# A planner's lag between dependent instructions of one engine, in a one-core hybrid decoder step

## The chip, the cores and the metric

The kernel runs on one core of one Trainium2 chip, as one launch. The metric is device time in microseconds (us), and the median of a few runs counts. Engine names are those of the profile: PE is TensorE's matmul side and PEld its weight loads, DVE is VectorE, ACT ScalarE, POOL GpSimd, SP SyncE; SPq is the queue on which SP issues its DMAs.

## The reference: what is computed

One layer of a decoder step for a prompt of 1024 tokens and 8 single-token samples, width 1024. The stream is normalised and modulated (adaLN), projected by `w_in` into parts, and sent to two groups of heads:

- an mLSTM with 4 heads of 128: a matrix memory carried over chunks of 128 tokens, each head's output normalised per token;
- sparse attention with 8 query heads of 64 and 2 key-value heads, in three branches (compressed blocks, the top 16 selected blocks, a window of 512), each a masked softmax with a relative-position bias, merged by sigmoid gates.

```python
parts, gate = adaln_project(x_p, c_prompt, w_ada, b_ada, w_in, b_in)
hm, (C_p, n_p, m_p) = mlstm_mixer(qm, km, vm, om, im, fm, m_norm_g, carry0, M_CHUNK)
ha = nsa_prompt(qa, cmp_p, slc_p, win_p, ga, cmp_params, rel_bias)
mix = concatenate([hm * silu(zm), ha * silu(za)], axis=-1)
x_p = layer_norm(DEEPNORM_ALPHA * x_p + gate * (mix @ w_out + b_out), ln_g, ln_b)
```

The samples go the same way against paged caches of 2048 rows each. Besides both streams the kernel returns the new key-value rows and the mLSTM's states.

## The kernel before

All of it is one program. Its stages overlap: the compression of the samples' cache, adaLN and normalisation (0 to 155 us of the span); the input projection, 35 blocks of up to 128 columns, each a matmul in three parts of split float32 (tile `mm`, from 110 to 914 us), which also serves as filler between other work; the samples' attention (232 to 363 us); the prompt's attention in 32 units (352 to 790 us); the four mLSTM heads (504 to 913 us); the output projection in 8 tiles of 128 tokens (from 914 us).

**The order is written by a planner, in Python, while the program is built.** Every piece of work is a generator, a *lane*, with a rank. `Lanes.run` (L326) takes, at each turn, the first lane in rank whose next step is ready by the planner's PE clock plus `SLACK` (0.2 us, L138), or else the one ready soonest, and lets it emit one step. The instructions then stand in that order in each engine's queue; an engine does not overtake, and waits by semaphore where a result isn't there yet. The planner's clocks never reach the chip; only the order does, and a few choices of engine: `sooner` (L506) gives an operation to the engine whose clock (plus a stated cost) is lowest, as in `sooner((V, 0.6), (G, 1.2))` for the products and the low halves of the output tiles (`mix_load`, L2355, and `split`, L518).

`Plan.note` (L247) keeps those clocks, one for each of PE, DVE, ACT, POOL and DMA (SP's queue). An instruction starts at the latest of its engine's clock and its waits. One kind of wait is read after write: for each part of a tile that it reads, the end of whatever wrote it, plus a lag given by `after` (L218): `LAG` of the writer's engine plus `TO` of the reader's. A step's readiness for PE is the latest `after(e, "PE")` of what it emitted (`step_end`), or the end of named tiles. A DRAM tile counts as one part, and a DMA that reads it waits for the DMAs that wrote it. The costs of an instruction are formulas: 0.069 us + n/960 for most DVE operations of n elements, 0.15 us + (n-1)/475 or /195 on POOL.

Steps that are named below:

- `mlstm_norm` (L1568), run 8 times (`mn00` to `mn31`): on DVE a chain of 13 instructions on `den`, `mst`, `mmv` and `mva` after the head's `nd`; then a reciprocal square root (`rsqrt_steps`, L475), 15 instructions on POOL for seven of the runs and 12 on DVE for the last; then `mva` and `nd` on DVE, PE transposes of `nd`, and `qm`.
- `finish` (L2233), run 9 times: the last layer norm, with a reciprocal square root of 9 instructions on DVE (`rs_v`, `rs_y`, `rs_t`, `frs`).
- DRAM tiles as ways between steps: `ud` to `ur` (`bias_tables`, L1790), `gpd` to `gate` (`out_gate`, L2267), and `mxd` and `gtd` to `mix` (`mix_load`).

Of the kernel before, what the change touches and what calls it, by code (L numbers as in the profile page):

```python
# [143 lines left out]
class Plan:  # L144
# [2 lines left out]

    LAG = {"PE": 0.2, "ACT": 0.15, "DVE": 0.13, "POOL": 0.08, "DMA": 0.0}
    TO = {"PE": 0.07, "POOL": 0.03}
    TICK = 10.24 / 3  # L150

    def __init__(self):
# [12 lines left out]
    def pe_cost(self, t, op, out, ins):  # L165
# [6 lines left out]
        else:  # L172
            cyc, passes = max(2 * n, 2 * m), 2
        tick = int(t / self.TICK)
        full = self.columns.get(tick - 1, 0) >= 3060
# [42 lines left out]
    def after(self, e, kind):  # L218
        return e[0] + self.LAG[e[1]] + self.TO.get(kind, 0.0)

# [26 lines left out]
    def note(self, kind, op, a, kw):  # L247
        aps = [x for x in a if isinstance(x, bass.AP)] + [x for k, x in kw.items() if isinstance(x, bass.AP)]
        out = kw.get("out", a[0] if a else None)
        outs = [out] + ([kw["accum_out"]] if "accum_out" in kw else [])  # L250
        if "in_offset" in kw and kw["in_offset"] is not None:
            aps.append(kw["in_offset"].ap)
        ins = list(aps)
        for o in outs:
            ins.pop(next(i for i, x in enumerate(ins) if x is o))
        eng = kind
        waits = [(self.clock[kind], kind, "")]
        for x in ins:
            for c in self.cells(x):
                for e in self.wrote.get(c, ()):  # L260
                    if not (kind == "PE" and e[1] == "PE"):
                        waits.append((self.after(e, kind), e[1], c))
        for x in aps:
            if x.space == PSUM or any(x is o for o in outs):
                for c in self.cells(x):
                    waits += [(self.after(e, kind), k, c) for k, es in self.used.get(c, {}).items() if k != kind
                              for e in es]
        load = kind == "DMA" or op == "indirect_dma_start"
        if load and len(self.begun[kind]) >= 8:
            waits.append((self.begun[kind][-8][0], "RING", ""))  # L270
        t = max(w[0] for w in waits)
        if load:
            size = out.free_size() * 4 * out.partition_size() / 360.0e3
            run = min(x.ap[-1][1] if x.ap[-1][0] == 1 else 1 for x in [out] + ins)
            if run < 128 and kind == "DMA":
                size *= 2
            self.clock[kind] = t + (1.04 if kind == "POOL" else 0.475)
            eng = "DMA"
            e = [0.0, eng]
            self.transfer(self.clock[kind] + 0.65, size, e)  # L280
            self.begun[kind].append(e)
        else:
            c = self.cost(kind, op, t, out, ins, len(outs) > 1)
            e = [t + c, kind]
            eng = kind
            self.clock[kind] = t + c
            self.step_end = max(self.step_end, self.after(e, "PE"))
        for x in outs:
            for c in self.cells(x):
                self.wrote[c] = (self.wrote.get(c, []) if eng == "DMA" else [])[-7:] + [e]  # L290
        for x in aps:
            for c in self.cells(x):
                u = self.used.setdefault(c, {})
                u[eng] = (u.get(eng, []) if eng == "DMA" else [])[-7:] + [e]
# [2176 lines left out]
```

## Time and profile before

| | |
|---|---|
| median of 3 runs | 1039.39 us (1038.61 to 1039.49) |
| the profiled execution | 1039.46 us, span 1037.6 us, mean granted TensorE clock 0.967 |
| PE busy | 959.7 us, 92% of the span |
| DVE, ACT, POOL busy | 717.2, 530.2, 286.5 us |
| chain that ended last | PE 57%, DVE 11%, DMA 4% of the span |

Span and busy times come from one profiled execution; 1.9 us lie around its span. The granted clock is 1.00 where TensorE ran at 2.4 GHz all the time and 0.50 where it ran at 1.2 GHz. A row of the view by stages gives each engine's busy time in that stretch, with the number of instructions in brackets; a row of the timeline gives start, length, engine, operation and tiles (out<-in), and in square brackets how long the engine had been idle and what released it.

### The profile page before, as it was taken

What the parts mean: (1) busy time and instruction counts of PE and PEld (TensorE: products, weight loads), DVE (VectorE), ACT (ScalarE), POOL (GpSimd) and SP (SyncE); (2) the same over time, 40 slices, a digit from 0 to 9 for tenths busy, and PEclk for the clock granted to TensorE, in tenths of its full rate; (3) what the DMA queues carried; (4) which work ended last, traced back from release to release, by engine and by line L of the source; (5) the groups of instructions that cost most, each with busy time, mean ns of one, the idle gap of its engine ahead of it and who ended that gap; (6) DMA issues with size and microseconds to landing.
All of it is one profiled execution on the core that took longest, in us unless ns stands there. A gap on an engine that the chain in (4) does not pass through costs nothing.

```text
span 1037.6 us, 20058 instructions
## 1 busy us (share of the span) xinstructions
PE 959.7 (92%) x7338; PEld 864.9 (83%) x7338; DVE 717.2 (69%) x2266; ACT 530.2 (51%) x1329; POOL 286.5 (28%) x362
## 2 busy tenths in 40 slices
PE   4997899999999989999999999999999899989990
PEld 3786897989888889899999998899998889967780
DVE  4859864072323477789777788878784738999996
ACT  3557752143344656676667786666773321231111
POOL 6216423111453000110131001131012524253563
PEclk9988899999999989999999999999999989989996
DMA  8943419413698715311105111012102326479502
GB/s 329 408 189 117 148 70 361 151 50 118 221 326 286 216 55 165 111 57 37 47 11 157 29 47 38 25 36 74 47 33 85 113 65 191 142 264 362 168 22 81
DMA packets 85334, 141.42 MB, mean 136 GB/s; under 512 B 11657, under 2 KB 58286, under 8 KB 85108
## 3 DMA queue, kind: packets, MB, share of 16 engines
q1 hardware_dynamic: 76020, 106.59, 31.2%
q0 software_dynamic: 9216, 33.56, 9.0%
q8 instruction: 58, 0.95, 0.4%
q14 instruction: 40, 0.33, 0.1%
HBM read 117.73 MB, written 28.15 MB: 141 GB/s over the span
## 4 chain that ended last, share of the span: by engine, by line
PE 57%; DVE 11%; DMA 4%; issue 2%; POOL 2%; ACT 1%; POOLq 0%; SPq 0%; DVEq 0%; ACTq 0%
PE mm L308 27%; PE sc L308 13%; PE tp L308 9%; PE oo L308 7%; DVE xr L308 2%; DMA wof<-in_w_out 1%; DMA pgs<-in_cache_slc_kv,idx 1%; DVE smp L308 1%; DVE lnst L308 1%; DVE rs_t L308 1%; POOL wol L308 1%; DMA mg<-mgd 1%; DVE mixl L308 1%; DMA pgs<-in_cache_win_kv 1%; DVE rs_y L308 0%
## 5 line engine op out<-in xcount | busy, mean ns | idle before, releaser
L308 PE MATMUL mm<-hh,wh 128*128 128x344 f32 (+1 forms) x840 | 286.3, 341 | 0.0
L308 PE MATMUL mm<-hl,wh 128*128 128x344 f32 (+1 forms) x840 | 270.4, 322 | 0.0
L308 PE MATMUL mm<-hh,wl 128*128 128x344 f32 x816 | 262.6, 322 | 0.0
L308 POOL TENSOR_TENSOR wl<-wf,wh 128x1024 fp32r<-128x1024 f32 (+1 forms) x35 | 82.5, 2356 | 505.0 <-ACT wh L308 389.6
L308 PEld LDWEIGHTS mm<-hh,wh 128*128 128x128 f32 (+1 forms) x840 | 158.8, 189 | 12.1 <-issue 10.5
L308 PEld LDWEIGHTS mm<-hl,wh 128*128 128x128 f32 (+1 forms) x840 | 158.9, 189 | 0.7
L308 PEld LDWEIGHTS mm<-hh,wl 128*128 128x128 f32 x816 | 155.1, 190 | 0.0
L308 PE MATMUL oo<-pt,VT 128*64 128x128 f32 x1056 | 70.1, 276 | 0.0
L308 PE MATMUL sc<-kst,qs 128*128 128x448 f32 (+6 forms) x208 | 69.5, 343 | 0.3 <-DVE pt L308 0.3
L308 PE MATMUL sc<-kst,ql 128*128 128x448 f32 (+6 forms) x208 | 65.5, 325 | 0.0
L308 PEld LDWEIGHTS oo<-pt,VT 128*64 128x64 f32 x1056 | 58.1, 137 | 6.4 <-issue 5.2
L308 DVE COPY pt<-tp 128x512 f32<-128x512 f32 (+1 forms) x87 | 54.8, 645 | 9.9 <-PE tp L308 9.7
L308 ACT ACTIVATE pw<-pw,nbs 128x64 f32<-128x64 f32 (+2 forms) x112 | 54.6, 489 | 12.6 <-DVE tot L308 6.4
L308 ACT ACTIVATE pt<-tp 128x512 f32<-128x512 f32 (+1 forms) x73 | 39.8, 558 | 40.6 <-PE tp L308 40.4
L308 ACT ACTIVATE pa<-pa,nbs 128x384 f32<-128x384 f32 (+1 forms) x88 | 50.9, 580 | 14.6 <-DVE pa L308 12.4
L308 ACT ACTIVATE xh<-tp 128x512 fp32r<-128x512 f32 x64 | 38.0, 595 | 35.2 <-PE tp L308 34.9
L308 DVE TENSOR_TENSOR xl<-tp,xh 128x512 fp32r<-128x512 f32 x64 | 42.8, 679 | 14.3 <-ACT xh L308 14.0
L308 PE MATMUL tp<-KA,pgx 128*128 128x128 f32 x256 | 43.3, 293 | 2.8 <-ACT pgx L308 1.9
L308 ACT ACTIVATE ti<-sc,PKT 128x129 f32<-128x129 f32 x28 | 10.3, 369 | 67.3 <-DVE cx L308 67.3
L308 ACT ACTIVATE pp<-pp,nbs 128x64 f32<-128x64 f32 (+3 forms) x72 | 32.2, 449 | 22.7 <-DVE nbs L308 21.3
L308 PE MATMUL sc<-xl,w1h 128*128 128x256 f32 x128 | 38.3, 299 | 5.0 <-DVE xl L308 5.0
L308 PEld LDWEIGHTS sc<-kst,qs 128*128 128x128 f32 x208 | 39.8, 191 | 3.3 <-DVE pt L308 1.0
(506 smaller groups left out, 2285.0 us busy)
## 6 DMA issues: line engine op xcount, KB each, us to landing
wf<-in_w_blk SPq DMA_DIRECT2D x34, 512.0 KB
wada<-in_w_ada SPq DMA_DIRECT2D x24, 512.0 KB
wof<-in_w_out SPq DMA_DIRECT2D x16, 512.0 KB
xt<-in_x_prompt SPq DMA_DIRECT2D x8, 512.0 KB
pgs<-in_cache_win_kv SPq DMA_DIRECT2D x8, 512.0 KB
qf<-qtd SPq DMA_DIRECT2D x32, 128.0 KB
mix<-mxd SPq DMA_DIRECT2D x16, 256.0 KB
mix<-gtd SPq DMA_DIRECT2D x16, 256.0 KB
```

The source lines that it names most:

```text
L308: return f(*a, **kw)
```

## The change

The planner gets a table `OWN`, and the read-after-write wait of an instruction on its own engine's result is counted with it in place of `LAG` and `TO`:

```diff
     LAG = {"PE": 0.2, "ACT": 0.15, "DVE": 0.13, "POOL": 0.08, "DMA": 0.0}
     TO = {"PE": 0.07, "POOL": 0.03}
+
+    OWN = {"ACT": 0.1, "DVE": 0.09, "POOL": 0.08}
...
         for x in ins:
             for c in self.cells(x):
                 for e in self.wrote.get(c, ()):
-                    if not (kind == "PE" and e[1] == "PE"):
+                    if e[1] != kind:
                         waits.append((self.after(e, kind), e[1], c))
+                    elif kind in self.OWN:
+                        waits.append((e[0] + self.OWN[kind], kind, c))
```

In the code before, the wait on the engine's own result is counted too, by `after`: 0.15 us for ACT, 0.13 us for DVE, 0.08 + 0.03 = 0.11 us for POOL. It becomes 0.10, 0.09 and 0.08 us. For PE none is counted, before or after. A DMA that reads what a DMA wrote had its wait counted with a lag of 0; DMA is not in `OWN`, so the planner now counts no wait there. No instruction is added or removed, and the semaphores on the chip follow the data as before.

## Rows read from the trace of the kernel before

**Rows 1.** Busy time by stage: stretch, its length, engines, PE's granted clock, DMA.
```profile
815.00:830.00 15.00, 10.82 (x64) 10.32 (x63) 11.17 (x22) 5.07 (x9) 9.30 (x18) 0.88 0.03 10
830.00:845.00 15.00, 15.00 (x93) 14.98 (x92) 4.33 (x11) 0.00 (x0) 2.21 (x1) 0.90 0.23 75
845.00:860.00 15.00, 12.46 (x97) 11.64 (x96) 8.59 (x35) 7.16 (x15) 4.16 (x5) 0.79 0.42 121
915.00:925.00 10.00, 6.69 (x19) 4.79 (x18) 9.80 (x18) 3.25 (x4) 6.97 (x3) 0.67 0.80 254
940.00:1012.00 72.00, 72.00 (x344) 56.33 (x343) 67.95 (x129) 12.91 (x16) 36.92 (x17) 1.00 0.51 169
```

**Rows 2.** Waits of PE: engine, tile <- releaser: us in total, times, longest.
```profile
PE tp L308 <- DVE nd L308: 5.9, 2, 4.2
PE oo L308 <- DVE gx L308: 3.1, 3, 1.5
PE sc L308 <- DVE vs L308: 3.0, 1, 3.0
PE tp L308 <- DVE d L308: 2.5, 1, 2.5
```

**Rows 3.** Timeline of DVE: four that don't depend on each other, then a chain.
```profile
1.20 0.34 DVE L308 TENSOR_SCALAR m<-io 128x1 f32<-128x1 int32 x4
...
1003.06 0.14 DVE L308 TENSOR_SCALAR rs_v<-fmv 128x1 f32<-128x1 f32 x1
1003.24 0.15 DVE L308 TENSOR_SCALAR rs_y<-rs_v 128x1 int32<-128x1 int32 x1
...
1004.96 0.16 DVE L308 SCALAR_TENSOR_TENSOR fnm<-fmv,frs 128x1 f32<-128x1 f32 x1
```

**Rows 4.** Timeline of POOL in the reciprocal square root of one `mlstm_norm`.
```profile
822.27 1.14 POOL L308 TENSOR_TENSOR rs_t<-rs_t,rs_v 128x4 f32<-128x4 f32 x1
823.50 0.23 POOL L308 TENSOR_SCALAR rs_t<-rs_t 128x4 f32<-128x4 f32 x1
823.81 0.20 POOL L308 TENSOR_TENSOR rs_y<-rs_t,rs_y 128x4 f32<-128x4 f32 x1
...
826.10 0.20 POOL L308 TENSOR_TENSOR mva<-rs_t,rs_y 128x4 f32<-128x4 f32 x1
```

**Rows 5.** Timeline of DVE around the same `mlstm_norm`.
```profile
812.90 1.83 DVE L308 SCALAR_TENSOR_TENSOR den<-nd 128x4 f32<-128x4 f32 x1
814.76 2.32 DVE L308 TENSOR_TENSOR den<-den,PKT 128x4 f32<-128x4 f32 x1
...
826.33 1.20 DVE L308 TENSOR_TENSOR mva<-mva,den 128x4 f32<-128x4 f32 x1 [2.98 <-POOL mva L308]
```

**Rows 6.** Timeline of PE, its transposes of `nd` in two runs of `mlstm_norm`.
```profile
827.97 1.25 PE L308 MATMUL tp<-KA,nd 128*128 128x128 f32 x4 [4.18 <-DVE nd L308]
...
912.27 0.84 PE L308 MATMUL tp<-KA,nd 128*128 128x128 f32 x3 [1.72 <-DVE nd L308]
```

**Rows 7.** Waits of SP's queue on a DMA's landing, where that DMA wrote DRAM.
```profile
SPq L308 <- DMA ud<-ut: 2.7, 1, 2.7
SPq L308 <- DMA gtd<-to: 2.0, 1, 2.0
SPq L308 <- DMA gpd<-smp: 0.9, 1, 0.9
SPq L308 <- DMA qtd<-qt: 0.8, 1, 0.8
```

**Rows 8.** Waits of POOL on the loads of the output tiles.
```profile
POOL mix L308 <- DMA mix<-gtd: 9.5, 6, 3.3
```

**Rows 9.** Groups by form: low halves of the output tiles on DVE and on POOL.
```profile
L308 DVE TENSOR_TENSOR mixl<-mix,mixh 128x512 fp32r<-128x512 f32 x8 | 14.3, 1812 | 0.0
L308 POOL TENSOR_TENSOR mixl<-mix,mixh 128x512 fp32r<-128x512 f32 x8 | 14.2, 1784 | 9.1 <-ACT mixh L308 6.4 <-PE mm L308 2.7
```

## The prediction

> **What bounds the kernel now.** The first view is busy time by stage. From 940 to 1012 us PE is busy for all of its 72 us, and so it is over most of the span; time is lost where PE stands still, and after it where PE runs at the lower of its two clocks [rows 1]. The stretches shown are the ones to look at: between 815 and 860 us PE is idle for 4.18 + 2.54 us and its granted clock is 0.88, 0.90 and 0.79, and between 915 and 925 us it is idle for 3.3 us at 0.67. The second view, PE's waits, says for whom it stands still: the longest after the start are for `nd`, the normalised mLSTM output (5.9 us in two waits), then for `gx`, `vs` and `d`, all of them ends of small chains on DVE [rows 2]. The third is the timeline of these chains [rows 3 to 6]. The kernel is bound by PE, and what the planner can win or lose is in how its order covers such chains. The change touches nothing else: no instruction comes or goes, only the planner's clocks, and through them the order and the choices of engine.
>
> **Is the plan nearer to the chip with the new numbers?** On DVE, four instructions on one element that don't depend on each other took 0.34 us together [rows 3]; the last of them ends one instruction's length after its start (0.15 us is the length of such a one in the chain), so their starts lie (0.34 - 0.15)/3 = 0.06 us apart. In the chain the first two, dependent, start 0.18 us apart. Dependence costs 0.12 us there. The plan's lag was 0.13 us and becomes 0.09 us: it was 0.01 too long and becomes 0.03 too short. Over the whole chain, from 1003.06 to 1004.96 us, nine starts took 1.90 us. The plan counts 0.07 us for each such instruction: eight of the nine steps are dependent and one isn't (`rs_v` needs no `rs_y`), so 9 x 0.07 + 8 x 0.13 = 1.67 us before and 9 x 0.07 + 8 x 0.09 = 1.35 us after. On POOL nine steps from 823.50 to 826.10 us took 2.60 us [rows 4]. The plan's formula gives 0.165 us for each of three tensor-scalar and 0.156 us for each of six tensor-tensor instructions on 4 elements, 1.43 us; with nine lags of 0.11 that is 2.42, with 0.08 it is 2.15 us. Both chains were counted a little short and are now counted shorter by 0.3 us. ACT has hardly a chain of its own, and its 0.05 us is left at nothing; an ACT result that PE or DVE reads keeps its lag.
>
> The Trainium skill, "VectorE: DVE Perf Modes", section "The DRAIN you can't avoid", says that each DVE operation empties its pipeline before the next starts and that a semaphore between them "costs nothing extra". By that rule a lag of one's own would be no lag at all, the smaller number would be the truer one, and the change would bring the plan closer to the chip. The rows disagree for these small operations (0.06 against 0.18 us); it gets a rival of its own below.
>
> **What the shift does, step by step.**
>
> *The norm chains.* One `mlstm_norm` has 9 dependent steps on DVE (`den` on `nd`, two more on `den`, four aggregates, two on `mva`), 12 on POOL, and one more on DVE. The plan counts 9 x 0.04 + 12 x 0.03 + 0.04 = 0.76 us less for it, in seven runs; in the eighth, all on DVE, 0.8 us. So the transposes of `nd` come ready in the plan 0.8 us earlier and stand earlier among PE's matmuls by up to that. Where PE already waits for them, this adds to the wait: 4.18 us and 1.72 us, two of eight runs [rows 6]. The first shows why the plan was short there: the two first steps took 1.83 and 2.32 us, the `mva` after POOL 1.20 us, and a POOL step before its plain ones 1.14 us [rows 4, 5], which no lag counts. PE waits there with its queue behind it, so an added wait is lost in full: 2 x 0.8 = 1.6 us. In the other six runs PE has projection matmuls before and behind, and the shift costs nothing; without that cover it would be 0.8 us each.
>
> *The other waits of PE for chains.* Three for `gx` have one dependent DVE step each, `vs` about one and `d` about four [rows 2]: 8 x 0.04 = 0.3 us.
>
> *DMA.* Before, the plan held SP's clock until a write to DRAM had landed; now it doesn't. The queue on the chip still waits: 2.7, 2.0, 0.9 and 0.8 us [rows 7]. So `ur`, `mix`, `gate` and `qf` are due in the plan that much too early. `ur` has no reader that near. For `gate` and the first `mix` the wait falls on POOL, which stood 9.5 us for such loads already [rows 8] and was busy for 6.97 of 10 us in that stretch [rows 1]; behind a blocked POOL stand the halves of `w_out` that PE needs. Bounds: nothing, if the order stays as it is, to 2.0 + 0.9 = 2.9 us, if both waits pass on to PE. A gain is possible too, as work behind these loads is no longer put off; by the same 2.9 us. The nearest row is POOL's wait, which PE's did not follow, so I take 0.
>
> *Everything else.* Each shift of a few hundredths can turn a choice of the next lane or of an engine, and from there on the order differs. This has no sign of its own. Its size is bounded by the places where order can win or lose: 6.7 us of idle time and 0.12 x 15 + 0.10 x 15 + 0.21 x 15 = 6.5 us of clock between 815 and 860 us, and as much again is open if new holes of that kind arise.
>
> **Sum.** The two terms are 1.6 + 0.3 = 1.9 us at most, and nothing at least if the matmuls before these transposes stay the same. I take the middle, 1.0 us, since the matmuls come in groups and a shift of 0.8 us moves a group or doesn't. 1039.46 (span 1037.6 and 1.9 around it) + 1.0 = 1040.4 us; the profiled execution stands 0.07 us over the median of the runs, so the two can be compared directly. A difference under 0.2%, 2.1 us, can't be told from none.
>
> **Rivals.**
>
> *Faster: a hole closes.* If the lanes fall so that PE has matmuls while the third head's norm runs, 4.18 us of idle go and with them the lowered clock of 815 to 845 us, 1.8 + 1.5 us [rows 1]: 7.5 us, to 1032; half of it gives 1035.7. I put it at 1034. For it: the hole is there, and seven other runs of the same chain cost PE 1.7 us together [rows 2, 6]. Against: it is caused by slow instructions that the plan doesn't know, and the plan now counts these chains shorter still.
>
> *Slower: DVE takes over the output stage.* From 940 to 1012 us DVE is busy for 67.95 of 72 us, so 4.05 us are free [rows 1]. With 8 `finish` chains of 8 dependent steps, a few more around each (some 12 x 0.04 = 0.5 us a tile), its plan clock runs early, and `sooner` needs only 0.6 us to turn a choice. Low halves are shared 8 to 8 at 1.81 us on DVE and 1.78 us on POOL [rows 9]. Three that turn to DVE add 5.4 us to it. Two (3.6 us) would still fit in the free time; from the third on DVE sets the pace. With half of the free time usable that is 5.4 - 2.0 = 3.4 us, and with the 1.6 us of the norm chains 1044.5. Against: POOL's lags shrink too.
>
> *The order hardly changes.* The lag was counted already and only gets smaller, so the change may do nothing of what it is called: 1039.4.
>
> *The plan gets truer.* If a dependent step really cost next to nothing more than a free one, the waits for chains would shrink by what I add: 1039.46 - 1.9 = 1037.6, and one wait like the 1.72 us with it, 1036. The 0.12 us measured above speaks against it.
>
> **Chances.** The forecast 0.37 (its own range 1036.5 to 1044.5: of it 0.04 faster, 0.20 the same, 0.13 slower); a hole closes 0.32, faster; DVE takes over 0.23, slower; the order stays 0.05, the same; the plan gets truer 0.03, faster. That is 0.39 faster, 0.25 the same, 0.36 slower. The range must hold most of both sides: down to the closed hole and 2 us more (1030), up to DVE's case and as much again as it adds (1050).
>
> **What would show it.** Right: in the changed profile PE's waits for `nd` are some tenths of a microsecond to 1.6 us longer in total, DVE's chain still has 0.18 us from start to start, SP's queue still waits for `ud`, `gtd` and `gpd`, and the 8 to 8 share of the low halves moves by two at most. Wrong on the faster side: PE has no wait over 2 us between 815 and 860 us and the clock stays near 1.00 there. Wrong on the slower side: PE idle between 940 and 1012 us, with DVE busy throughout. If the median moves by 5 us or more while the waits for `nd`, the shares and the waits of SP's queue are as before, the reasoning by chains is wrong altogether, and the turned choices elsewhere decide.

## The result, and the profile after

The changed kernel takes 1049.36 us (median of 6 runs, 1045.90 to 1052.81), the kernel before beside it 1039.44 us (6 runs, 1038.61 to 1042.49). The ratio is 1.0098, with a 95% interval of 1.0077 to 1.0118: it is slower by about 10 us, where 1 us was forecast. The profiled execution of the changed kernel took 1045.90 us (span 1044.1 us against 1037.6 us), the lowest of its six, so this profile shows 6.5 us of the loss and nothing of the rest. A second profile of the changed kernel below, on another chip, has a span 9.7 us longer than one of the old order (`after_again` and `control`, 1062.7 and 1053.0 us).

Busy time by stage, in the changed kernel; the columns are those of [rows 1].

```profile
815.00:830.00 15.00, 14.61 (x97) 13.95 (x97) 10.24 (x31) 4.49 (x11) 7.80 (x18) 1.00 0.21 58
830.00:845.00 15.00, 15.00 (x102) 14.98 (x102) 5.07 (x11) 0.80 (x1) 2.40 (x1) 1.00 0.23 76
845.00:860.00 15.00, 12.41 (x115) 11.83 (x114) 9.49 (x36) 7.17 (x15) 5.00 (x9) 1.00 0.40 119
...
915.00:925.00 10.00, 1.54 (x4) 1.03 (x5) 9.80 (x19) 3.17 (x3) 5.50 (x2) 0.65 0.36 121
...
940.00:1012.00 72.00, 65.94 (x299) 50.21 (x297) 63.06 (x120) 12.98 (x17) 34.18 (x17) 0.99 0.56 184
```

Two things happened. The hole at 815 us closed (PE busy for 14.61 us instead of 10.82) and the granted clock stayed at 1.00 up to 860 us, where it was 0.88, 0.90 and 0.79. But between 915 and 925 us PE worked for 1.54 us only, where it had worked for 6.69 us, and between 940 and 1012 us it stood idle for 6.06 us, where it had stood for none.

PE's waits in the changed kernel (tile <- releaser: us in total, times, longest):

```profile
PE sc L312 <- DVE wol L312: 6.6, 1, 6.6
PE sc L312 <- ACT mixh L312: 6.1, 1, 6.1
PE oo L312 <- DVE gx L312: 3.1, 3, 1.5
PE sc L312 <- DVE vs L312: 3.0, 1, 3.0
...
PE tp L312 <- DVE d L312: 2.6, 1, 2.6
PE sc L312 <- ACT woh L312: 2.6, 1, 2.6
...
PE tp L312 <- DVE nd L312: 0.4, 1, 0.4
```

The waits for `nd` have all but gone, from 5.9 to 0.4 us [rows 2]. Those for `gx`, `vs` and `d` are as they were. New at the top are `wol`, the low half of a scaled piece of `w_out`, `mixh`, the high half of an output tile, and `woh`, the high half of such a piece. The waits for `woh` and `wol` end at 916.86 and 923.97 us, at the entrance of the output projection; the one for `mixh` ends at 1012.05 us, before the last output tile.

**The ledger of the profiles.** PE's rows give these times: the last projection matmul ends at 911.7 us (914.0 before), the last matmul of the output tiles at 1026.1 (1013.6), the span at 1044.1 (1037.6). So the changed kernel is 2.3 us ahead when the output stage begins. From there to the last output matmul it needs 114.4 us instead of 99.6: PE is idle for 15.5 instead of 3.3 us, and busy for 98.9 instead of 96.3 us at a mean granted clock of 0.93 instead of 0.97. After that matmul it needs 18.0 instead of 24.0 us, because DVE, which went on while PE stood, has 9.1 us of work left there instead of 14.2. The sum: -2.3 + 14.8 - 6.0 = 6.5 us, the difference of the spans. PE's busy time over the whole span did not change (959.5 and 959.7 us).

**The entrance, row by row.** The timeline of the changed kernel at the loads of `w_out` and around 915 us (start, length, engine, operation, tiles; "x2" is two in one row):

```profile
901.65 1.71 SPq L312 DMA_DIRECT2D wof<-in_w_out  x2
...
908.15 2.27 SPq L312 DMA_DIRECT2D wof<-in_w_out  x4
...
912.36 2.22 DVE L312 TENSOR_TENSOR wol<-wof,woh 128x1024 fp32r<-128x1024 f32 x1 [1.13 <-ACT woh L312]
914.50 1.21 DVE L312 TENSOR_TENSOR wof<-wof,gate 128x1024 f32<-128x1024 f32 x1
914.83 3.10 POOL L312 TENSOR_TENSOR wof<-wof,gate 128x1024 f32<-128x1024 f32 x1 [1.33 <-DMA wof<-in_w_out]
915.64 2.66 DVE L312 SCALAR_TENSOR_TENSOR tz<-tz,zv 128x344 f32<-128x344 f32 x1
915.75 1.06 ACT L312 ACTIVATE woh<-wof 128x1024 fp32r<-128x1024 f32 x1 [2.55 <-DVE wof L312]
...
917.89 2.61 POOL L312 TENSOR_TENSOR wof<-wof,gate 128x1024 f32<-128x1024 f32 x1
918.34 2.54 DVE L312 SCALAR_TENSOR_TENSOR to<-to,tz 128x344 f32<-128x344 f32 x1
...
920.90 0.33 SPq L312 DMA_DIRECT2D gtd<-to  x1
...
922.68 2.36 DVE L312 TENSOR_TENSOR wol<-wof,woh 128x1024 fp32r<-128x1024 f32 x2
```

and the same steps in the kernel before:

```profile
901.20 3.29 SPq L308 DMA_DIRECT2D wof<-in_w_out  x5
...
915.42 0.51 DVE L308 SCALAR_TENSOR_TENSOR tz<-tz,zv 128x344 f32<-128x344 f32 x1
...
915.96 0.52 DVE L308 SCALAR_TENSOR_TENSOR to<-to,tz 128x344 f32<-128x344 f32 x1
916.50 0.33 SPq L308 DMA_DIRECT2D gtd<-to  x1
...
916.67 3.34 POOL L308 TENSOR_TENSOR wol<-wof,woh 128x1024 fp32r<-128x1024 f32 x1 [4.54 <-ACT woh L308]
...
917.73 4.73 DVE L308 TENSOR_TENSOR MXS<-MXS,gsm 128x8 f32<-128x8 f32 x4
```

`tz` and `to` put the last block of the projection away. Before, they took 0.51 and 0.52 us and had ended (916.48 us) when POOL began a product (916.67 us). After, POOL is in two products of `w_out` pieces at that time, and the same two take 2.66 and 2.54 us. The planner counts 0.069 + 344/960 = 0.43 us for each, whatever POOL does. The `wol` behind them in DVE's queue had its input at 916.81 (915.75 + 1.06) and started at 922.68: that is PE's wait of 6.6 us. But DVE is held in the kernel before as well, just afterwards: its four operations on `MXS` take 4.73 us beside POOL's `wol` and the product behind it, and 0.39 us in the changed kernel (at 920.99 us). That is 4.3 us lost before and 4.2 us after (5.20 for `tz` and `to` instead of 1.03). The hold-up is not new; what differs is what stands behind it. And `gtd<-to` leaves at 920.90 instead of 916.50 us, 4.4 us later, with every output tile's loads behind it on SP's queue. POOL's waits for these loads rose from 9.5 us [rows 8]:

```profile
POOL mix L312 <- DMA mix<-gtd: 23.4, 6, 8.1
```

The chain that ended last (start, length, what) shows the two again, DVE's pair and then a load, with PE between them, and goes on with DVE:

```profile
918.34 2.55 DVE to L312
923.97 5.44 PE sc L312 x14
...
941.18 6.90 DMA mix<-gtd
948.10 0.69 DVE mix L312
```

**The other end of the stage.** The wait for `mixh` stands some 90 us after that for `wol`:

```profile
1010.24 1.24 ACT L312 ACTIVATE xr<-xr,fnm,frs 128x1024 f32<-128x1024 f32 x1 [7.80 <-DVE fnm L312]
1011.39 1.13 ACT L312 ACTIVATE mixh<-mix 128x512 fp32r<-128x512 f32 x2
...
1012.05 0.79 PE L312 MATMUL sc<-woh,mixh 128*128 128x512 f32 x1 [6.11 <-ACT mixh L312]
```

These two `mixh` had their input when DVE's last products `mix` ended at 994.24 us. They stood in ACT's queue behind an operation of a `finish`, which waited 7.80 us for `fnm`, the end of that layer norm's chain on DVE. So DVE was behind by then. It lost the time earlier: the stages of the changed kernel,

```profile
926.00:950.00 24.00, 24.00 (x108) 17.97 (x107) 10.26 (x13) 2.85 (x4) 7.03 (x5) 0.95 1.03 348
950.00:1012.00 62.00, 55.94 (x249) 43.50 (x247) 58.63 (x114) 12.35 (x16) 32.68 (x15) 0.99 0.48 154
```

and of the kernel before:

```profile
926.00:950.00 24.00, 24.00 (x105) 19.40 (x104) 21.44 (x31) 5.99 (x8) 6.74 (x5) 1.00 1.10 354
```

Between 926 and 950 us DVE worked for 10.26 us instead of 21.44, mostly waiting for `mixh` (4.4 us), `woh` (4.3 us) and the load of a `mix` (4.0 us); from 950 us on it had 3.4 us free of 62. Of PE's 15.5 us of idle time, 9.2 thus lie at the entrance (3.3 before) and 6.1 before the last tile, where the kernel before has none.

### The profile page after: what moved, and what is told of

It is laid out like the page before. It is cut to its first block, busy times and chain, and to the rows that moved or that the text cites. A ratio compares the mean times of both kernels' runs of the same rounds, so it can differ in the third digit from the quotient of the medians.

```text
span 1044.1 us, 20090 instructions
## 1 busy us (share of the span) xinstructions
PE 959.5 (92%) x7338; PEld 861.1 (82%) x7338; DVE 712.5 (68%) x2266; ACT 527.0 (50%) x1328; POOL 289.3 (28%) x363
## 4 chain that ended last, share of the span: by engine, by line
PE 65%; DVE 22%; DMA 5%; ACT 3%; issue 3%; POOL 1%; POOLq 0%; SPq 0%; DVEq 0%; ACTq 0%
PE mm L312 30%; PE sc L312 15%; PE tp L312 12%; PE oo L312 8%; DVE xr L312 2%; DVE lnst L312 2%; DMA wf<-in_w_blk 1%; DVE rs_t L312 1%; DMA pgs<-in_cache_slc_kv,idx 1%; DVE xl L312 1%; DVE Cst L312 1%; DVE smp L312 1%; DMA pg<-in_cache_cmp_kv,idx 1%; DVE rs_y L312 1%; DVE mix L312 1%
## 5 line engine op out<-in xcount | busy, mean ns | idle before, releaser
L312 PE MATMUL sc<-xh,w1h 128*128 128x256 f32 x128 | 42.4, 332 | 0.0
```

What stands on the lines that cost most here:

```text
L312: return f(*a, **kw)
```

## The experiments

They ran on three other chips, on which the kernel before takes 1053.6 to 1054.9 us. All ratios are to the kernel before, run beside them on the same chip. There its output stage is as long as in the first result (123.7 and 123.6 us from the last projection matmul to the end), while the last projection matmul ends some 15 us later. All times in the table but the ratios come from one profiled execution each, which need not be a typical one: that of `late` is the lowest of its ten, that of `after_w7v` the highest of its eleven.

| kernel | last projection matmul | from it to the end | PE idle until the last output matmul | ratio, 95% interval |
|---|---|---|---|---|
| before (first chip) | 914.0 | 123.6 | 3.3 | |
| after (first chip) | 911.7 | 132.4 | 15.5 | 1.0098, 1.0077 to 1.0118 |
| after_again | 930.4 | 132.3 | 15.1 | 1.0116, 1.0083 to 1.0149 |
| control | 929.3 | 123.7 | 3.3 | 0.9979, 0.9959 to 1.0000 |
| lag_only | 931.3 | 134.3 | 16.6 | 1.0108, 1.0050 to 1.0167 |
| dma_only | 924.1 | 129.6 | 13.8 | 1.0042, 1.0013 to 1.0071 |
| measured | 930.2 | 132.8 | 12.5 | 1.0105, 1.0073 to 1.0137 |
| eps | 932.8 | 122.0 | 6.7 | 1.0007, 0.9980 to 1.0033 |
| early | 931.1 | 123.7 | 3.3 | 0.9997, 0.9975 to 1.0018 |
| late | 922.9 | 131.7 | 15.2 | 1.0059, 1.0037 to 1.0081 |
| after_v | 933.7 | 128.5 | 13.0 | 1.0053, 1.0030 to 1.0076 |
| after_w7 | 930.0 | 129.2 | 11.8 | 1.0081, 1.0051 to 1.0112 |
| after_w7v | 933.3 | 123.9 | 6.8 | 1.0010, 0.9988 to 1.0033 |
| before_v | 923.3 | 133.7 | 19.2 | 1.0051, 1.0034 to 1.0068 |

The second column is to be read coarsely: control, late and before_v lie up to 6.4 us apart, and up to 3.8 us of that is there at 789 us, where their orders are still the same. The third column is the steadier one, and it goes with the fourth. It goes with DVE's idle time, too: from the last projection matmul to the last output matmul DVE stands idle for 5 to 10 us in the five kernels that lose nothing (before 5.5, control 5.1, early 5.0, eps 8.7, after_w7v 10.2) and for 12.5 to 21.2 us in the others (after 19.9). And the late wait is in all the slower ones: 78 to 106 us behind the last projection matmul PE waits 3.6 to 9.6 us for `mixh` or `mixl` (after_w7v 5.8, eps 2.3), and not at all in before, control and early.

**Which part of the change?** The change has two parts: three shorter lags, and a wait of DMA on DMA that is no longer counted. `lag_only` does the first alone and `dma_only` the second; `control` writes the old numbers into the new table, which gives the order of before instruction for instruction. The edits:

```diff
 control   OWN = {"ACT": 0.15, "DVE": 0.13, "POOL": 0.11, "DMA": 0.0}
 lag_only  OWN = {"ACT": 0.1, "DVE": 0.09, "POOL": 0.08, "DMA": 0.0}
 dma_only  OWN = {"ACT": 0.15, "DVE": 0.13, "POOL": 0.11}
```

In dma_only, early, late and the kernels with edits at `w_out`, the output lane also names all pieces of `w_out` that it waits for, which by itself leaves the order of before as it is.

> The code of the changed kernel with the numbers of before (0.15, 0.13, 0.11 us, and the DMA wait counted with 0): the program is that of before, instruction by instruction. All theories: no difference, the ratio's interval holds 1. It shows how far two equal programs lie apart, and gives a profile to set beside those of the same chip: from the last projection matmul to the end some 123 us, with 3 to 4 us of PE idle up to the last output matmul.

> The three shorter lags alone; the planner counts the wait of a DMA on a DMA's write as before. Its order is that of the changed kernel up to some 800 us and differs from it in the output projection's entrance. Early plan (the time grows with how much too short DVE's lag is): 1047 to 1052 us, all of the loss. Luck of one place (the order at the entrance of the output projection, where the halves of w_out are made, decides): anything from 1039 to 1052 us, and whatever it is shows as PE's idle time between 900 and 930 us. DMA (the dropped DMA wait does it): 1038 to 1041 us.

> The lags of before; only the wait of a DMA on a DMA's write is no longer counted. (The output lane also names all eight pieces of w_out that it needs, which leaves the order of the kernel before as it is.) The order is that of before up to about 900 us. Early plan: 1037.5 to 1041.5 us, no loss. DMA: 1045 to 1052 us. Luck of one place: anything from 1036 to 1050 us, seen in PE's idle time between 900 and 930 us.

The lags alone lose as much as the whole change. The dropped DMA wait alone loses 0.42% (4.4 us; 1.4 to 7.5 by the interval), which does not add to the other. Each part moves the output stage by itself to another order, and each of these is worse than the one of before. In `dma_only` the four computing engines keep the old order up to 937 us and only SP's queue differs earlier (from 818 us), and of PE's waits 5.1 us are for a `mixl` 90 us behind the last projection matmul.

**Is it the accuracy of the lag?** `measured` takes the lags that the traces show, 0.118 us for DVE; `eps` shortens every old lag by 0.002 us, which says nothing about the chip and only turns close choices.

```diff
 measured  OWN = {"ACT": 0.13, "DVE": 0.118, "POOL": 0.13, "DMA": 0.0}
 eps       OWN = {"ACT": 0.148, "DVE": 0.128, "POOL": 0.108, "DMA": 0.0}
```

> Lags of an engine on its own result set to what the trace of before shows from start to start over a free one: DVE 0.118, ACT 0.13, POOL 0.13 us; the DMA wait counted as before. Early plan: no slower than before, 1034 to 1040 us, since the plan is nearer to the chip. Luck of the order: unrelated to the lag's truth, anything from 1034 to 1050 us. DMA: 1038 to 1041 us.

> The lags of before, each shorter by 0.002 us (ACT 0.148, DVE 0.128, POOL 0.108), the DMA wait counted as before; the order first differs in PE's 3035th row of 6182. Early plan: 1037.5 to 1041.5 us, a twentieth of the change can't be seen. Luck of the order: the time scatters as it does for the change, anything from 1034 to 1050 us, over 2 us off in two of three such cases. DMA: 1038 to 1041 us.

These lags lose 1.05%, as much as the too short ones, with other waits: for `nd` 6.1 us in all (5.8 in control), and in the output stage for `nd`, a load and `mixl`, 4.0, 4.0 and 3.6 us. So the loss is not simply that the plan is too early. `eps` turned PE's order from its 3035th instruction on and changed nothing that can be measured, though PE idles 3.4 us more in the output stage.

**Where in the kernel?** `early` plans with the new numbers until the values of the prompt's attention are done (about 780 us) and with the old ones after it; `late` the other way round.

```diff
         yield from done("values", "mgd")
+        plan.OWN = <the other table>
```

> The changed planner up to the end of the attention's values (some 780 us), then the lags and the DMA wait of before. Entrance (the loss arises in the output projection, from the numbers that the planner uses there): 0 to -0.3% against before, as the changed kernel reached its last projection matmul 2.3 us sooner. Inherited (the order up to 780 us brings the loss with it): +0.8 to +1.1%. Luck of the order: the output stage gets a third order, with anything from 118 to 134 us after the last projection matmul.

> The planner of before up to the end of the attention's values (some 790 us), then the changed one. Entrance: +0.7 to +1.2%, all of the loss. Inherited: -0.2 to +0.3%, none of it. Luck of the order: anything from -0.5 to +1.2%, with the output stage at 118 to 134 us; the order differs from the kernel with the DMA part alone too, so the two needn't agree.

PE's waits from 880 us on, in `early`:

```profile
PE sc L312 <- POOL wol L312: 2.9, 1, 2.9
PE tp L312 <- DVE nd L312: 1.7, 1, 1.7
PE sc L312 <- ACT woh L312: 0.4, 1, 0.4
```

and in `late`:

```profile
PE sc L312 <- DVE wol L312: 6.6, 1, 6.6
PE sc L312 <- ACT mixh L312: 5.7, 1, 5.7
PE sc L312 <- ACT woh L312: 2.6, 1, 2.6
```

`early` has the three waits of the kernel before, to 0.1 us, and loses nothing; `late` has those of the changed kernel and loses 0.59%. Everything that the new numbers changed before 780 us, the longest part of the kernel, is worth nothing that can be measured: the loss needs what they change after it. `late` shows part of that loss and not all that was expected of it (0.7 to 1.2%): its interval ends at 1.0081, where that of `after_again` begins at 1.0083. Why the rest is missing is open.

**What at the entrance?** Two things differ there in the rows of the first profiles: POOL's products beside DVE's operations, and the loads of `w_out`. SP issued five of these loads together at 901.20 us, and now issues two at 901.65 and four at 908.15 us. In SP's queue the four stand behind a write, `mxd<-qm`, that waited 4.3 us for `qm`. One of the pieces, w7, may be loaded only once w6 is done. `after_v` gives both products to DVE always; `after_w7` frees w7's load (in the kernel before this edit changes no computing engine's order, and on SP's queue it only swaps two of the five loads); `after_w7v` does both; `before_v` gives the products to DVE in the kernel before; `after_again` is the changed kernel, on the chip of `after_w7`, `after_w7v` and `before_v`. Each edit also deals the order anew from some point on: `after_w7` leaves that of the changed kernel at 908 us, `after_v` and `after_w7v` at 804 us.

```diff
 after_v, after_w7v, before_v
-            sooner((V, 1.2), (G, 2.3)).tensor_tensor(w, w, og["gate"], op=ALU.mult)
+            V.tensor_tensor(w, w, og["gate"], op=ALU.mult)
...
-            sooner((V, 1.2), (G, 2.3)).tensor_tensor(wol[k], w, fb(woh[k]), op=ALU.subtract)
+            V.tensor_tensor(wol[k], w, fb(woh[k]), op=ALU.subtract)
 after_w7, after_w7v
-        lanes.add(6, out_weights((7,), "w6"), "w7")
+        lanes.add(6, out_weights((7,), "smlstm"), "w7")
```

> The changed kernel, with the products that make the halves of w_out (tiles wof and wol) always on DVE and never on POOL. Contention (at the entrance DVE's operations on two SBUF tensors are held while POOL runs a 2.4 us operation: tz and to at 2.66 and 2.54 us, where they take 0.5 us alone): these two are back at 0.5 us, PE's waits of 6.6 and 2.6 us for the halves shrink by half or more, and 4 us or more of the loss is gone, +0.2 to +0.6%. Luck of the order: no sign, -0.5 to +1.3%. DVE as the bound (four operations of 2.4 us on POOL become 1.2 us each on a DVE that is busy throughout): slower than the changed kernel, over +1.2%.

> The changed kernel itself on this chip, so that the three others have it beside them. If the loss belongs to the order and not to the chip, ratio 1.008 to 1.012 and the waits for wol and mixh of 5 to 7 us each, as in the first result; the share of the loss behind the last projection matmul is 8 to 9 us.

> The changed kernel, but the load of the last piece of w_out (w7) no longer waits for w6 to be finished; in the kernel before the same edit leaves every engine's order as it is. The orders of the changed kernel and of this one are the same up to PE's 5756th instruction of 6182. Theory 'late load': four pieces were loaded only at 908 us and made PE wait for their products, so with an earlier load PE's waits for wol (6.6 us) and mixh (6.1 us) shrink below 3 us each and the ratio to the kernel before falls from 1.010 to 1.004 or less. Theory 'contention': the products on POOL beside DVE's two-input operations make the waits, whenever the load comes, so the ratio stays at 1.008 to 1.012 and a wait of 5 us or more for wol stays. Theory 'favoured order': the order of the kernel before is simply good there and every other one loses some; ratio 1.003 to 1.010 and other names in the waits.

> The changed kernel with w7's load freed as well as both products of w_out's pieces always on DVE. 'Late load' and 'contention' together: the two edits add up, and the ratio falls from 1.010 to 1.000 to 1.003, below the 1.0053 of the products on DVE alone. 'Favoured order': no better than the products on DVE alone, 1.004 to 1.008, as DVE then makes PE wait for the low halves mixl.

> The kernel before with both products of w_out's pieces always on DVE; in its own order 5 of the 16 or so ran on POOL. 'Contention': two-input products on POOL hold DVE back here as well (an evacuation of 0.5 us alone took 4.7 us beside one), so this is as fast as the kernel before or up to 3 us faster, ratio 0.997 to 1.001. 'Favoured order': it loses as any other order of this stage does, ratio 1.003 to 1.008, through a new wait of PE for mixl or wol of 3 us or more.

PE's waits from 880 us on, in `after_v`:

```profile
PE sc L312 <- DVE mixl L312: 7.5, 2, 6.5
PE sc L312 <- DVE wol L312: 3.6, 1, 3.6
```

in `after_w7v`:

```profile
PE sc L312 <- DVE mixl L312: 5.8, 2, 4.8
...
PE sc L312 <- DVE wol L312: 0.6, 1, 0.6
```

and in `before_v`:

```profile
PE sc L312 <- ACT woh L312: 6.6, 1, 6.6
PE sc L312 <- ACT mixh L312: 4.2, 1, 4.2
```

`after_again` has the loss of the first result and its place (132.3 us from the last projection matmul on, 8.6 more than control), with the waits dealt a little otherwise: `mixh` 5.8, `woh` 4.7, `wol` 4.3 us. With the products off POOL `tz` and `to` are back at 0.51 and 0.52 us, as "contention" expected, but PE's waits for the halves, 9.2 us together (`wol` 6.6, `woh` 2.6), fall to 5.5 (3.6 and 1.9) and not by half; the wait for `mixh` at the last tile goes, and one of 6.5 us for `mixl` comes in its place, as DVE now has more to do. With w7's load freed as well, `wol` is nearly on time (0.6 us) and PE idles for 6.8 us instead of 15.1, 5.8 of it for `mixl` towards the end of the stage. This kernel keeps every new lag and loses nothing that can be measured: 1.0010 against 1.0116 for the changed kernel on the same chip, with intervals far apart. `after_w7` alone cannot be told from the changed kernel (1.0081, overlapping intervals), though its idle time is 3.3 us less.

So "late load" alone falls by its ratio, "contention" alone has the ratio that it expected of `after_w7` but not the wait (3.4 us for `wol`, and 7.2 us for `mixl`), and the two together have theirs in `after_w7v`, where "favoured order" (1.004 to 1.008) has not. But contention is no rule for this stage: `before_v`, which takes the same products off POOL in the old order, loses 0.51% and has the longest idle time of all, though no `tz`, `to` or `MXS` is held in it at the entrance (0.51, 0.52 and 0.16 us). The ratio that "favoured order" expected of it holds; its longest waits are for `woh` and `mixh` and not for `mixl` or `wol`. (The 4.7 us that its expectation gives for one evacuation are the row of four operations on `MXS`, two of them held for 2.3 us each.) With one order per edit, a lucky order is not excluded as the reason why `after_w7v` is as fast as before. None of the kernels is faster than the one before; `early`, `eps` and `after_w7v` equal it.

## Why the prediction was off

**What bounds the kernel: right up to the output stage, and half of the truth there.** PE is as busy as before over the span. But the chain that ended last leaves PE already in the kernel before, at 942.68 us, and from there to the end it runs mostly through DVE:

```profile
942.68 0.69 DVE xr L308
```

The prediction read 72 us of PE without a gap as "bound by PE" and gave DVE's 67.95 us there a place in a rival only. In the changed kernel DVE's 11 lost us between 926 and 950 us come back as PE's wait at the last tile and as the later end.

**The lag of DVE: right as a reading, and it did not matter.** Small operations in one chain of the changed kernel (timeline of DVE) still start 0.18 us apart:

```profile
951.83 0.15 DVE L312 TENSOR_SCALAR rs_v<-fmv 128x1 f32<-128x1 f32 x1
952.01 0.15 DVE L312 TENSOR_SCALAR rs_y<-rs_v 128x1 int32<-128x1 int32 x1
```

But `measured`, with about the lag that these rows give (0.18 - 0.07 us), is no better than the changed kernel.

**The norm chains, +1.6 at most: wrong in sign.** The waits for `nd` went from 5.9 to 0.4 us; in lag_only, with the same shorter lags, they are 2.0 us, and in `measured`, with a longer lag on POOL, 6.1 us. The step took the shift of 0.8 us as added to a wait in a fixed queue. The queue is not fixed: which projection matmuls stand before the transposes decides, and these were dealt anew. The "slow instructions that the plan doesn't know" have a cause in the rows, too, and it is the one found at the entrance: `den` took 1.83 and 2.32 us [rows 5] and ended at 814.73 and 817.08 us, within 0.03 us of the end of POOL's 2.4 us products of 812.28 and 814.63 us; `mva` (1.20 us) ended 0.02 us after POOL's operation of 826.25 us; POOL's step of 1.14 us [rows 4] ended 0.05 us after DVE's `wol` of 822.13 us. No run varied this, so it is a reading. "If the lanes fall so" of the rival that a hole closes is what happened, clock and all, and by luck: 2.3 us ahead at 912 us in the first profile. No ratio shows that this lead lasts: in the later profiles the changed kernel stood at 930.4 us there and control at 929.3.

**The other waits, +0.3: too small to matter.** `gx`, `vs` and `d` changed by 0.1 us in all.

**DMA, taken as 0: too small.** SP's queue still waits, as the prediction said:

```profile
SPq L312 <- DMA ud<-ut: 2.5, 1, 2.5
SPq L312 <- DMA gtd<-to: 2.1, 1, 2.1
```

But this part alone costs 4.4 us against an upper bound of 2.9; the interval, 1.4 to 7.5, holds both. The bound counted the waits on the chip and not the order that follows from them. The row on which the 0 rested, POOL's 9.5 us that PE did not follow, became 23.4 us. PE did not wait for these loads directly; DVE did, for 4.0 us, and through DVE and ACT this is part of the 6.1 us at the last tile.

**The failed step: "Everything else. ... This has no sign of its own."** The text added that "as much again is open if new holes of that kind arise", named 6.7 us of idle time as the size, and left it out of the sum, between terms of 1.6 and 0.3 us. The holes came: 12.2 us more of idle PE in the output stage and 2.6 us more of busy PE at the lower clock, of which 8.8 us are left at the end. It had a sign in that stage, too: [rows 1] show PE without a gap for 72 us beside a DVE at 94%, an order with little to win and much to lose (this is said with the result known). Six kernels came to another order of that stage through numbers of the planner alone, and five of them (the changed one, lag_only, dma_only, measured, late) lost 0.4 to 1.2%; eps lost nothing.

**The rival "DVE takes over the output stage": the right stage and side and half of its sign, another mechanism.** It put the loss at 940 to 1012 us, PE idle with DVE busy throughout, through low halves that turn to DVE. The halves moved by one, to POOL (groups by form):

```profile
L312 DVE TENSOR_TENSOR mixl<-mix,mixh 128x512 fp32r<-128x512 f32 x7 | 10.6, 1535 | 4.4 <-ACT mixh L312 4.4
L312 POOL TENSOR_TENSOR mixl<-mix,mixh 128x512 fp32r<-128x512 f32 x9 | 15.2, 1711 | 3.3 <-ACT mixh L312 3.3
```

so DVE got no more work. But PE was idle for 6.06 us there, behind a DVE that was busy for 58.63 of the 62 us from 950 us on: it had been kept waiting before, between 926 and 950 us. The other 9.2 us of PE's idle time lie at the entrance, which this rival did not name. The prediction's own condition for being wrong altogether came close to what is seen: 5 us or more, with shares and SP's waits as before (the waits for `nd` are not), and the turned choices decide. That the measured median lies inside the range is luck: its upper end was drawn for that rival, whose mechanism did not occur.

**What stays open.** Which single choice of the planner first led to the other entrance is not known; on paper DVE's lag alone turns the order from DVE's 46th instruction on, POOL's alone from PE's 3432nd on, and ACT's turns nothing. That POOL's products hold DVE back is in the rows of both kernels, but the experiments took the products off POOL, which gives DVE more work and another order, so the share of the hold-up apart from the late loads and from the order is not settled. That the time DVE lost between 926 and 950 us causes the wait at the last tile is read from the chain and the queues; no run changed it alone. Why the changed kernel's runs spread over 7 us on the first chip is not known.

## What to carry to other kernels

A small change of a number in a planner deals the order anew from there on: price it by the stage with the least slack left, as a loss, and not by the chains that the number is about. Where two engines are both nearly full, look at both: time that the second one loses early in the stage can come back as a wait of the first at its end. A truer number need not give a faster order while the plan leaves out a larger effect (here two engines that hold each other up, 2.6 us where it counts 0.43). Before such a number is judged, run its neighbours and a version that switches it half way: here these showed in four kernels that the accuracy was not the cause and which stage was.

## What the runs showed of the hardware

A DVE operation with two inputs in SBUF took five times as long beside a two-input operation of POOL: `tz` and `to`, 128x344, 0.51 and 0.52 us alone, 2.66 and 2.54 us beside POOL's two 128x1024 products, which took 3.10 and 2.61 us themselves against 2.42 us for one in the kernel before (906.13 us). The Trainium skill, "SBUF — State Buffer", section "SBUF: two separate sides", says why: such operations of DVE and of GpSimd share a pair of ports that one holds for its whole instruction while the other blocks. The rows agree: POOL's two end at 917.93 and 920.50 us, and DVE's two end 0.4 us after each. It goes the other way as well: POOL's first product began at 914.83 us beside a product of DVE's that ran until 915.71 us, and is the longer of the two.
